# A streaming encoder layer on one core: other waits and priorities in the first norm, and spatial products of the v rows stepped later

## Chip, core and metric

The kernel runs on one core of a Trainium2 chip, as one program. The metric is the device time of an execution in microseconds; the kernel before takes 1891.32 us (median of 3 runs, 1890.37 to 1892.46). A core has a matmul engine (TensorE, called PE in the profile), VectorE (DVE), ScalarE (ACT), GpSimd (POOL) and SyncE (SP), each with its own queue of instructions, which it works off in order. They meet through semaphores. Matmuls write to PSUM, of which the kernel holds eight tiles of one bank; the other engines empty them.

## What is computed

One inference step of one layer for 1024 prompt rows and 32 sample rows, all in float32. Cut to what matters:

```python
x = layer_norm(x, ln_in_g, ln_in_b)
f = swiglu(modulate(x, 0), ffn1_w1, ffn1_w3, ffn1_w2)
x = layer_norm(ALPHA * x + 0.5 * gate(0) * f, ln_g[0], ln_b[0])      # the first norm

proj = modulate(x, 1) @ w_in
xa, ga, us, vs = jnp.split(proj, [D_LRU, 2 * D_LRU, 2 * D_LRU + D_SG], axis=-1)
xc, new_hist = causal_conv(xa, conv_hist, conv_w, conv_b)
hl, h_last = rg_lru(xc, h0, lru_wa, lru_ba, lru_wx, lru_bx, lru_lambda)
ya = hl * jax.nn.gelu(ga)
vn = layer_norm(vs, sg_ln_g, sg_ln_b)
yb = spatial_gate(us, vn, sg_w, sg_b)                                # us * (tril(w_s) @ vn + b_s)
m = jnp.concatenate([ya, yb], axis=-1) @ w_out
x = layer_norm(ALPHA * x + gate(1) * m, ln_g[1], ln_b[1])

f = swiglu(modulate(x, 2), ffn2_w1, ffn2_w3, ffn2_w2)
x = layer_norm(ALPHA * x + 0.5 * gate(2) * f, ln_g[2], ln_b[2])
```

`modulate` and `gate` scale and shift by vectors that come from c. The spatial gate works on blocks of 128 rows, in four groups of 128 columns. Outputs are the rows, the states of the convolution and of the recurrence, and the normalised v rows of the sample.

## The kernel before

**Layout.** Activations lie transposed, 128 features on the partitions, eight feature blocks k, and the 1056 rows along the free side in three chunks: 384, 384 and 288 (`CH`, indices 0 to 2). A float32 product is made of three matmuls with a high part and a low part of each operand: high by high, high by low, low by high. `split` (L209) makes such a pair: ACT copies the high part (L210), DVE or POOL subtracts it to get the low part (L211). One k of one chunk, three matmuls, is called a group here.

**Order.** PE's instructions run in the order in which the Python code issues them. The other engines' instructions are ordered by a planner, which takes each engine's ready instruction of the highest priority by its own estimate of durations; the priority is the place in the program, and `high_priority(offset=n)` moves an instruction n places forward in it.

**Side work.** Work beside the main products is written as generators. `self.pe` is a clock that counts the planned length of the matmuls issued so far: columns / 2.4 ns, so 0.16 us for 384 columns and 0.12 for 288, times four for a plain float32 product. `go` (L156) registers a generator with a due time; a yielded number is the time until its next step. `poll` (L162) steps the generators that are due. It is called behind every group of the main products, and in the v rows behind each row tile (24 matmuls of 512 columns). `drain` (L173) steps one generator at once to its end, or, with `out=True` and a norm, until its modulated rows are issued.

**The first norm.** `last_f` issues the last products of the first feed-forward net chunk by chunk: per chunk eight sets of nine matmuls, each emptied by `add_gated` (L960 adds to the residual rows, L966 to the running total `tot`). Behind each chunk it registers `ln` (L1189) for it. `ln` has four steps, with the waits of `STEPS[(1, chunk)]` ahead of the first, the second and the third product:

- the product `psl<-tot,ones`, which sums over the features; DVE subtracts the mean (L1202)
- then, if the chunk before has issued its modulated rows, ACT squares in two halves into two `t` tiles (L1210), and DVE adds up the squares (L1213, L1215, L1218)
- the products `psl<-ones,t`, the variance; L562 on DVE and L563 on POOL make the inverse root, L1232 a diagonal of it
- the last product `psl<-tot,ones`; DVE scales the rows (L1241), ACT scales and shifts by the coefficients (L539, into the same two `t` tiles) and makes the high part `xh` (L546), DVE the low part `xl` (L549), in four pairs of feature blocks; the rows are spilled to DRAM

The second tuple of `STEPS` holds the priorities of these four groups of instructions.

**The mix.** `mix` (L1502) then issues, chunk by chunk (`chunkwise`, L1535, which drains the norm of a chunk ahead of its first product), the products ga 0 to 3 and xa 0: 40 groups of chunk 0, 40 of chunk 1, 40 of chunk 2. Behind them come xa 1 and xa 2 (`whole`), then the v rows, xa 3, and again chunk by chunk us 0 to 3, whose eviction multiplies with `zb` (L1531). The products of `w_out` (wo) follow. Beside all this the generator `lru` runs the convolution and the recurrence, long DVE instructions over 1060 columns, with gate products `psg`; it is drained behind chunk 0 of us.

**The v rows.** Nine row tiles, three per chunk: 24 matmuls each, and ACT copies the result into a tile of the tag `v0` (L1595; the profile calls the tile `v`). `sgv` (L1461) normalises the three tiles of a chunk (L1471 to L1475), then for each splits it into `vhl`, a tile of the tag `raw`, and behind a wait issues twelve products `psz` with the spatial weights and evicts them into `zb` (L1492, four instructions). For the sample's tile it also loads two rows (L1497) and stores vn (L1500), through SP. `sgv` of a chunk is drained behind the first row tile of the next chunk, ahead of its copy, and the last one ahead of us.

The `raw` tag has five buffers. They hold the weight tiles that SP loads from DRAM (L205), and the tiles of `sgv` and `lru`.

Of the kernel before, what the change touches and what calls it, by code (L numbers as in the profile page):

```python
# [12 lines left out]
F32 = mybir.dt.float32  # L13
# [6 lines left out]
P = 128  # L20
# [20 lines left out]
for _n, _w in _COLS:  # L41
# [18 lines left out]

STEPS = {
# [61 lines left out]
class Core:  # L123
# [1337 lines left out]
    def sgv(self, c, v0):  # L1461

        nc, V, S, G = self.nc, self.nc.vector, self.nc.scalar, self.nc.gpsimd
        mv = self.mixl.tile([P, 3, 2], F32, tag="vmv", name="vmv", bufs=2)
        rs = self.mixl.tile([P, 3, 2], F32, tag="vrs", name="vrs", bufs=2)
        c0 = CH[c][0]
        rows = [P if c * 3 + j < 8 else NS for j in range(3)]
        for j in range(3):
            n = rows[j]
            bs = self.mixl.tile([P, 6], F32, tag="vbs", name="vbs", bufs=2)  # L1470
            V.bn_stats(bs[:n], v0[j][:n])  # L1471
            V.bn_aggr(mv[:n, j, :], bs[:n])
            self.rsqrt(rs[:n, j, 0:1], mv[:n, j, 1:2])
            V.scalar_tensor_tensor(rs[:n, j, 1:2], mv[:n, j, 0:1], -1.0, rs[:n, j, 0:1], ALU.mult, ALU.mult)
            S.activation(v0[j][:n], v0[j][:n], AF.Identity, scale=rs[:n, j, 0:1], bias=rs[:n, j, 1:2])  # L1475
        yield 6.0
        for j in range(3):
            n = rows[j]
            vh = self.wpool.tile([P, 2, 512], F32R, tag="raw", name="vhl", bufs=RAWS)
            self.split(vh[:n, 0, :], vh[:n, 1, :], v0[j][:n])  # L1480
            yield 2.0
            ps = self.ps("psz")
            for g in range(4):
                gs = slice(g * P, (g + 1) * P)
                o = ps[:, g * P:g * P + n]
                wg = slice(g * P, g * P + n)
                self.mm(o, vh[:n, 0, gs], self.wt[:n, 0, wg], True, False)
                self.mm(o, vh[:n, 0, gs], self.wt[:n, 1, wg], False, False)
                self.mm(o, vh[:n, 1, gs], self.wt[:n, 0, wg], False, True)
            tk = c0 + j * P  # L1490
            for g in range(4):
                V.scalar_tensor_tensor(self.zb[:, g, tk:tk + n], ps[:, g * P:g * P + n], self.v("sg_g", g),  # L1492
                                       self.R[:, g, :n], ALU.mult, ALU.add)
            if n == NS:
                r = self.wpool.tile([P, 1024], F32, tag="raw", name="raw", bufs=RAWS)
                for q, nm in ((0, "sglg"), (1, "sglb")):
                    nc.sync.dma_start(r[:NS, q * 512:(q + 1) * 512], self.i[nm].partition_broadcast(NS))  # L1497
                V.tensor_tensor(v0[j][:n], v0[j][:n], r[:NS, 0:512], ALU.mult)
                V.tensor_tensor(v0[j][:n], v0[j][:n], r[:NS, 512:1024], ALU.add)
                nc.sync.dma_start(self.o["vn"], v0[j][:n])  # L1500

    def mix(self, ln1, es_a, es_mr):  # L1502
# [5 lines left out]
        def new_xab(f, pool, bufs):  # L1508
            x = pool.tile([P, 1064], F32, tag="l", name="xab", bufs=bufs)
            nc.gpsimd.memset(x[:, 0:3], 0.0)  # L1510
            nc.gpsimd.memset(x[:, 1062:1064], 0.0)
            hist = self.v("hist").rearrange("p (r f) -> p r f", f=4)
            V.tensor_copy(x[:, 1027:1030], hist[:, :, f])
            xabs[f] = x
# [20 lines left out]
        def chunkwise(items, before=None, after=None):  # L1535
            ws = []
            for c in range(3):
                if before:
                    self.drain(before[c], True)
                for j, it in enumerate(items):  # L1540
                    if c == 0:
                        ws.append(self.w_get(it))
                        if it[0] == "xa":
                            new_xab(it[1], self.mixr, 1)
                    ps = self.ps()
                    for k in range(K):
                        self.h_mm(ps, ws[j], c, k, k == 0, k == K - 1)
                    outs[it[0]](it[1], c, ps)
                    if c == 2:
                        self.w_rel()  # L1550
                if after:
                    after(c)

        def whole(it):
            w = self.w_get(it)
            if it[0] == "xa":
                new_xab(it[1], self.mixl, 7)
            ps = [self.ps() for _ in range(3)]
            for k in range(K):
                for c in range(3):  # L1560
                    self.h_mm(ps[c], w, c, k, k == 0, k == K - 1)
            self.w_rel()
            for c in range(3):
                outs[it[0]](it[1], c, ps[c])
# [12 lines left out]
        whole(("xa", 2))  # L1577
        self.drain(sgc)
        wv = [self.w_get(("vs", j)) for j in range(4)]
        sg = None  # L1580
        for c in range(3):
            v0 = []
            for j in range(3):
                n = P if c * 3 + j < 8 else NS
                ps = self.ps()
                for k in range(K):
                    h, l = (x[c][:, k, j * P:j * P + n] for x in (self.xh, self.xl))
                    wh, wl = wv[k // 2][k % 2][:, 0], wv[k // 2][k % 2][:, 1]
                    self.mm(ps[:n, :], h, wh, k == 0, False)
                    self.mm(ps[:n, :], h, wl, False, False)  # L1590
                    self.mm(ps[:n, :], l, wh, False, k == K - 1)
                if j == 0 and sg:
                    self.drain(sg)
                t = self.mixl.tile([P, 512], F32, tag="v0", name="v0", bufs=3)
                S.activation(t[:n], ps[:n, :], AF.Copy)  # L1595
                v0.append(t)
                self.poll()
            sg = self.go(self.sgv(c, v0))
        self.w_rel(8)
        whole(("xa", 3))  # L1600
        self.drain(sg)

        def to_x(c):
            self.drain(lru)
            c0, n = CH[c]
            for h, src in ((0, self.ya), (1, self.zb)):
                sl = slice(4 * h, 4 * h + 4)
                self.split(self.xh[c][:, sl, :], self.xl[c][:, sl, :], src[:, :, c0:c0 + n])

        chunkwise([("us", j) for j in range(4)], after=to_x)  # L1610
        es_l.close()
        es_mr.close()
        self.apool, self.es_a2 = self.pool("a2", side="left")
# [130 lines left out]
```

## Time and profile before

| | |
|---|---|
| median of 3 runs | 1891.32 us (1890.37 to 1892.46) |
| the profiled execution | 1891.25 us |
| its span, first to last instruction | 1889.4 us |
| mean granted TensorE clock | 0.99 |
| PE in `ps<-xh,wh` products, the largest group | 901.7 us, 3824 matmuls |
| the chain that ended last | PE 83%, DVE 9%, POOL 3%, ACT 3%, DMA 1% |

The profile is of one execution. A line is read as line, engine, operation, output <- inputs, count; times in a timeline are microseconds from the start of the span, followed by the length, and in brackets stands the idle time ahead of an instruction and what ended it. PE's busy time is modelled from matmuls that overlap, so a busy PE need not run at its full rate: the granted clock says at which it ran (1.00 is full). The part of the span that the change touches lies between 770 us, where chunk 0 of the last feed-forward products ends, and 1040 us, where wo begins.

### The profile page before, as it was taken

What the parts mean: (1) busy time and instruction counts of PE and PEld (TensorE: products, weight loads), DVE (VectorE), ACT (ScalarE), POOL (GpSimd) and SP (SyncE); (2) the same over time, 40 slices, a digit from 0 to 9 for tenths busy, and PEclk for the clock granted to TensorE, in tenths of its full rate; (3) what the DMA queues carried; (4) which work ended last, traced back from release to release, by engine and by line L of the source; (5) the groups of instructions that cost most, each with busy time, mean ns of one, the idle gap of its engine ahead of it and who ended that gap; (6) DMA issues with size and microseconds to landing.
All of it is one profiled execution on the core that took longest, in us unless ns stands there. A gap on an engine that the chain in (4) does not pass through costs nothing.

```text
span 1889.4 us, 28312 instructions
## 1 busy us (share of the span) xinstructions
PE 1830.2 (97%) x11295; PEld 1793.0 (95%) x11295; DVE 1334.5 (71%) x2362; ACT 683.3 (36%) x1200; POOL 557.1 (29%) x416
## 2 busy tenths in 40 slices
PE   6989999999999999989999999999999999999997
PEld 3889999999999999979789999999999999999996
DVE  7889888878888866962977467965645554565667
ACT  5551332233223223344554437222232233223224
POOL 2493434233333424022000000133333233423410
PEclk9999999999999999989899999999999999999999
DMA  7351353445445433222011401111111112012102
GB/s 294 123 182 65 126 187 131 139 154 173 147 139 179 147 110 123 90 76 78 3 51 39 168 23 46 45 56 35 45 67 46 45 45 68 23 45 68 45 1 92
DMA packets 51028, 175.70 MB, mean 93 GB/s; under 512 B 7504, under 2 KB 10192, under 8 KB 50128
## 3 DMA queue, kind: packets, MB, share of 16 engines
q1 hardware_dynamic: 31984, 102.77, 16.1%
q10 hardware_dynamic: 18912, 71.11, 10.9%
q8 instruction: 89, 1.46, 0.3%
q14 instruction: 43, 0.35, 0.1%
HBM read 165.13 MB, written 8.74 MB: 92 GB/s over the span
## 4 chain that ended last, share of the span: by engine, by line
PE 83%; DVE 9%; POOL 3%; ACT 3%; DMA 1%; issue 1%; SPq 0%; ACTq 0%; DVEq 0%; POOLq 0%
PE ps L153 80%; PE psl L153 1%; DVE xl L549 1%; POOL s L801 1%; DVE wh L211 1%; DVE xa L960 1%; PE psz L153 1%; POOL tx L804 1%; PE psa L153 1%; DVE araw L714 1%; POOL s L802 1%; DMA araw<-ada 1%; PE psg L153 0%; POOL raw L242 0%; ACT wh L210 0%
## 5 line engine op out<-in xcount | busy, mean ns | idle before, releaser
L153 PE MATMUL ps<-xh,wh 128*128 128x384 f32 (+1 forms) x3824 | 901.7, 319 | 3.0 <-ACT xh L546 1.8
L153 PEld LDWEIGHTS ps<-xh,wh 128*128 128x128 f32 x3824 | 662.1, 188 | 6.6 <-ACT xh L546 2.0
L153 PE MATMUL ps<-xl,wh 128*128 128x384 f32 (+1 forms) x1912 | 608.2, 318 | 4.2 <-DVE xl L549 4.2
L210 ACT ACTIVATE wh<-raw 128x512 fp32r<-128x512 f32 x452 | 281.1, 628 | 587.7 <-PE ps L153 462.9
L153 PE MATMUL ps<-g,wh 128*128 128x384 f32 (+1 forms) x2808 | 459.6, 323 | 3.0 <-ACT g L210 1.3
L153 PEld LDWEIGHTS ps<-g,wh 128*128 128x128 f32 x2808 | 453.1, 188 | 5.0 <-ACT g L210 1.5
L211 DVE TENSOR_TENSOR wh<-raw,wh 128x512 fp32r<-128x512 f32 x283 | 215.1, 764 | 223.4 <-ACT wh L210 218.1
L153 PEld LDWEIGHTS ps<-xl,wh 128*128 128x128 f32 x1912 | 359.8, 188 | 7.6 <-DVE xl L549 6.5
L211 POOL TENSOR_TENSOR wh<-raw,wh 128x512 fp32r<-128x512 f32 x169 | 248.3, 1471 | 387.3 <-ACT wh L210 385.9
L960 DVE SCALAR_TENSOR_TENSOR xb<-ps,gt,xb 128x384 f32<-128x384 f32 (+1 forms) x352 | 151.4, 484 | 79.4 <-PE ps L153 65.1
L714 DVE SCALAR_TENSOR_TENSOR araw<-araw,cb 128x1024 f32<-128x1024 f32 x112 | 161.1, 1444 | 15.1 <-DMA araw<-ada 11.0
L153 PE MATMUL ps<-tx,wh 128*128 128x384 f32 x912 | 167.1, 338 | 0.0
L240 POOL TENSOR_TENSOR raw<-raw 128x512 f32<-128x512 f32 x38 | 54.5, 1434 | 365.7 <-DVE wh L211 361.0
L153 PEld LDWEIGHTS ps<-tx,wh 128*128 128x128 f32 x912 | 159.8, 188 | 0.0
L960 DVE SCALAR_TENSOR_TENSOR xa<-ps,gt,xa 128x384 f32<-128x384 f32 (+1 forms) x320 | 135.1, 479 | 8.5 <-PE ps L153 8.4
L210 ACT ACTIVATE g<-s 128x384 fp32r<-128x384 f32 (+1 forms) x126 | 61.3, 493 | 168.3 <-DVE s L675 168.2
L852 DVE TENSOR_TENSOR s<-s,ps 128x384 f32<-128x384 f32 x152 | 83.8, 551 | 41.4 <-PE ps L153 39.7
L211 DVE TENSOR_TENSOR g<-s,g 128x384 fp32r<-128x384 f32 (+1 forms) x126 | 93.5, 748 | 21.8 <-ACT g L210 20.8
L563 POOL TENSOR_TENSOR r<-r,half 128x3 f32<-128x3 f32 x8 | 7.1, 888 | 303.9 <-DVE r L562 303.9
L153 PE MATMUL ps<-T,wh 128*128 128x384 f32 x456 | 85.6, 335 | 0.0
L675 DVE TENSOR_TENSOR s<-s 128x384 f32<-128x384 f32 x76 | 59.0, 777 | 32.4 <-ACT s L902 31.4
L242 POOL TENSOR_TENSOR raw<-raw 128x512 f32<-128x512 f32 x38 | 55.7, 1465 | 87.3 <-DVE wh L211 85.9
(246 smaller groups left out, 1684.9 us busy)
## 6 DMA issues: line engine op xcount, KB each, us to landing
raw<-wst SPq DMA_DIRECT2D x156, 512.0 KB, 3.8
araw<-ada ACTq DMA_DIRECT2D x112, 512.0 KB, 3.5
wnat<-ada SPq DMA_DIRECT2D x8, 512.0 KB, 10.2
raw<-ada SPq DMA_DIRECT2D x8, 512.0 KB, 3.6
xt<-x SPq DMA_DIRECT2D x7, 512.0 KB, 8.4
araw<-wst ACTq DMA_DIRECT2D x6, 512.0 KB, 4.5
sp<-xa ACTq DMA_DIRECT2D x2, 1536.0 KB, 5.7
xb<-sp ACTq DMA_DIRECT2D x2, 1536.0 KB, 10.3
```

Source lines behind the costliest of these rows:

```text
L153: self.nc.tensor.matmul(out, a, b, start=start, stop=stop, skip_group_check=True)
L210: self.nc.scalar.activation(dst_h, src, AF.Copy)
L211: (e or self.nc.vector).tensor_tensor(dst_l, src, dst_h.bitcast(F32), ALU.subtract)
L240: G.tensor_tensor(a["A21"], a["A11"], a["A21"], ALU.subtract)
L242: G.tensor_tensor(a["A22"], a["A22"], a["A21"], ALU.subtract)
L549: V.tensor_tensor(xl, tmp, xh.bitcast(F32), ALU.subtract)
L675: self.nc.vector.tensor_tensor(s, s, x, ALU.mult)
L714: V.scalar_tensor_tensor(raws[n], raws[n], 1.0, cb, ALU.mult, ALU.mult, accum_out=self.mod[:, m, f, v:v + 1])
L801: e.tensor_tensor(r, x[i][:, k, :].bitcast(F32), y[i][:, k, :].bitcast(F32), op)
L802: e.tensor_tensor(t, t, u, ALU.add)
L852: self.mark = V.tensor_tensor(out, x, ps[:, :n], ALU.add)
L960: self.mark = V.scalar_tensor_tensor(X[:, m, a + o:a + o + w], ps[:, o:o + w], self.gt[:, s, m, v:v + 1], X[:, m, a + o:a + o + w], ALU.mu ...
```

## The change

It has four parts.

- `STEPS[(1, 1)]`: the variance of chunk 1 waits 14 instead of 12, and the subtraction of its mean has the priority offset 0 instead of 30.
- `STEPS[(1, 2)]`: the mean of chunk 2 waits 15 instead of 6, its last product 4.0 instead of 2.5.
- `sgv`: the wait behind the norm is 9.0 instead of 6.0, and the wait between a split and its products 4.5 instead of 2.0.
- `mix`: the tag `v0` has six buffers instead of three. `sgv` of a chunk is no longer drained behind the first row tile of the next chunk; from the third chunk on, that of the chunk before the last one registered is. Nothing is drained behind xa 3; instead `chunkwise` drains `sgv` of a chunk ahead of the us products of that chunk.

```diff
@@ -60,8 +60,8 @@
     (1, 0): ((1.2, 12.0, 4.0), (0, 30, 0, 0), 0),
-    (1, 1): ((4.0, 12.0, 4.0), (30, 30, 0, 30), 0),
-    (1, 2): ((6.0, 12.0, 2.5), (0, 0, 30, 0), 0),
+    (1, 1): ((4.0, 14.0, 4.0), (0, 30, 0, 30), 0),
+    (1, 2): ((15.0, 12.0, 4.0), (0, 0, 30, 0), 0),
@@ -1473,12 +1473,12 @@
             S.activation(v0[j][:n], v0[j][:n], AF.Identity, scale=rs[:n, j, 0:1], bias=rs[:n, j, 1:2])
-        yield 6.0
+        yield 9.0
         for j in range(3):
             n = rows[j]
             vh = self.wpool.tile([P, 2, 512], F32R, tag="raw", name="vhl", bufs=RAWS)
             self.split(vh[:n, 0, :], vh[:n, 1, :], v0[j][:n])
-            yield 2.0
+            yield 4.5
             ps = self.ps("psz")
@@ -1577,7 +1577,7 @@
-        sg = None
+        sgs = []
         for c in range(3):
@@ -1589,17 +1589,15 @@
-                if j == 0 and sg:
-                    self.drain(sg)
-                t = self.mixl.tile([P, 512], F32, tag="v0", name="v0", bufs=3)
+                if j == 0 and len(sgs) > 1:
+                    self.drain(sgs[-2])
+                t = self.mixl.tile([P, 512], F32, tag="v0", name="v0", bufs=6)
                 S.activation(t[:n], ps[:n, :], AF.Copy)
                 v0.append(t)
                 self.poll()
-            sg = self.go(self.sgv(c, v0))
+            sgs.append(self.go(self.sgv(c, v0)))
         self.w_rel(8)
         whole(("xa", 3))
-        self.drain(sg)
@@ -1607,7 +1605,7 @@
-        chunkwise([("us", j) for j in range(4)], after=to_x)
+        chunkwise([("us", j) for j in range(4)], before=sgs, after=to_x)
```

## The prediction

> **What bounds the kernel now.** I read the page first, then the waits of TensorE, then windows around the longest of them, then the timelines of the engines inside those windows.
>
> ```profile
> span 1889.4 us, 28312 instructions
> PE 1830.2 (97%) x11295; PEld 1793.0 (95%) x11295; DVE 1334.5 (71%) x2362; ACT 683.3 (36%) x1200; POOL 557.1 (29%) x416
> ```
>
> PE is busy 97% of the span, so only two things can be won: its 59 us of idle time (1889.4 - 1830.2), and stretches in which it is "busy" but slow. The waits of PE between 700 and 1060 us (total, times, longest) show what lies in the stage that the change touches:
>
> ```profile
> PE psl L153 <- DVE tot L966: 4.5, 1, 4.5
> PE psz L153 <- DVE vhl L211: 3.7, 3, 2.7
> PE ps L153 <- DVE xl L549: 2.4, 3, 1.3
> PE psz L153 <- ACT vhl L210: 0.8, 1, 0.8
> PE psl L153 <- DVE t L1218: 0.7, 1, 0.7
> ```
>
> The first, third and fifth belong to the first norm, the others to the v rows. The windows (length; busy of PE, PEld, DVE, ACT, POOL; granted clock; DMA share; GB/s) show that each long wait costs a second time:
>
> ```profile
> 801.84:812.54 10.70, 8.32 (x44) 7.04 (x42) 10.70 (x22) 8.06 (x10) 5.93 (x3) 1.00 0.15 50
> 812.54:817.05 4.51, 0.00 (x0) 0.00 (x0) 4.51 (x6) 0.03 (x1) 3.68 (x3) 0.87 0.32 116
> 817.05:826.35 9.30, 9.30 (x31) 9.01 (x31) 3.27 (x5) 0.49 (x1) 0.85 (x1) 0.51 0.18 56
> 927.82:933.21 5.39, 1.88 (x16) 1.60 (x14) 5.28 (x10) 4.41 (x6) 0.00 (x0) 0.88 0.01 2
> 933.21:942.00 8.79, 8.79 (x32) 7.92 (x33) 8.10 (x18) 1.34 (x2) 0.55 (x1) 0.50 0.00 0
> ```
>
> After the idle 4.51 us the clock stands at 0.51 for 9.30 us, which is worth 9.30 x 0.49 = 4.6 us; after the psz waits at 0.50 for 8.79 us, 4.4 us. The three xl waits (2.4 us, spread over the first window) left it at 1.00. DVE is full in the first two windows: there the norm waits for VectorE's queue, not for its own length.
>
> **The norm, step by step.** The planner's clock counts 0.16 us for a matmul of 384 columns and 0.12 for 288; the chip takes (next start minus start, over 24) 0.173:
>
> ```profile
> 749.80 4.32 PE L153 MATMUL ps<-tx,wh 128*128 128x384 f32 x24
> 753.96 2.25 PE L153 MATMUL ps<-T,wh 128*128 128x384 f32 x12
> 801.84 0.34 PE L153 MATMUL ps<-xh,wh 128*128 128x384 f32 x1
> 836.71 0.35 PE L153 MATMUL ps<-xh,wh 128*128 128x384 f32 x1
> ```
>
> The last two rows start chunks 0 and 1 of the ga/xa products: 34.87 us for 120 matmuls, which need 20.8 us plus about 1.3 for the norm's own products. So 12.8 us are lost here; 2.4 + 4.5 + 4.6 = 11.5 of them are named above, and the other 1.3 are slow restarts behind the short waits, which I leave to the low end of the range.
>
> *Priority 30 to 0 for the mean subtraction (L1202) of chunk 1.* These DVE and ACT rows show what it did:
>
> ```profile
> 797.80 1.75 DVE L1202 SCALAR_TENSOR_TENSOR xa<-psl,xa 128x1536 f32<-128x1536 f32 x1
> 799.83 1.75 DVE L1202 SCALAR_TENSOR_TENSOR xa<-psl,xa 128x1536 f32<-128x1536 f32 x1
> 802.81 0.95 DVE L549 TENSOR_TENSOR xl<-t,xh 128x768 fp32r<-128x768 f32 x1
> 807.25 0.95 DVE L549 TENSOR_TENSOR xl<-t,xh 128x768 fp32r<-128x768 f32 x1
> 803.79 1.49 ACT L1210 ACTIVATE t<-xa 128x1536 f32<-128x1536 f32 x1 [2.99 <-DVE xl L549]
> 808.23 1.49 ACT L1210 ACTIVATE t<-xa 128x1536 f32<-128x1536 f32 x1 [0.66 <-DVE xl L549]
> ```
>
> Both L1202 go ahead of the second and fourth xl of chunk 0, though their own squares (L1210) cannot start before exactly these: the two "t" tiles are free only when xl has read them. So the priority gained the norm nothing and made PE wait. Without it the second xl can follow the first L1202 at 799.5, the fourth can be done near 804, and the squares near 802.3 and 805.5. Nothing is added; 2.4 us go.
>
> *Waits.* In planner time the mean of chunk 1 stands 4.68 us into the products of chunk 2, and chunk 0 of ga/xa starts at 9.28. Its variance moves from 16.68 to 18.68: behind group 20 of 40 (a group is three matmuls, 0.48), which is 801.84 + 60 x 0.173 = 812.2 us. Its last product, 4.0 later, comes behind group 27 or 28, at about 816.8. The mean of chunk 2, which now waits 15 instead of 6, comes behind group 30 (818.4); its variance behind group 14 or 15 of chunk 1, its last product (4.0 instead of 2.5) behind group 22. The total that PE waited for ended at 817.0:
>
> ```profile
> 781.18 0.55 DVE L1218 TENSOR_TENSOR t<-t,t 128x384 f32<-128x384 f32 x1
> 815.18 1.45 DVE L1218 TENSOR_TENSOR t<-t,t 128x384 f32<-128x384 f32 x1
> 816.55 0.44 DVE L966 TENSOR_TENSOR tot<-tot,xa 128x288 f32<-128x288 f32 x1
> 806.61 6.64 POOL L211 TENSOR_TENSOR wh<-raw,wh 128x512 fp32r<-128x512 f32 x3 [18.30 <-ACT wh L210]
> 813.21 3.01 POOL L211 TENSOR_TENSOR wx<-raw,wx 128x512 fp32r<-128x512 f32 x2
> ```
>
> At 818.4 it is there even if DVE is no faster: 4.5 and the 4.6 of slow clock go. What is late next is the variance at 812.2, which needs L1218 of chunk 1. From squares done at 805.5 three sums follow; at the slow lengths that they have while POOL splits weights (L1218: 1.45 against 0.55) they take about 4.5 us, so 810, or 813 with two totals between them. I take no stall; the other end is the rival below.
>
> *The next chunk comes sooner.* Chunk 0 now ends near 823.9, and its cover over the modulation of chunk 1 shrinks. Before, the last product and the four xl stood so:
>
> ```profile
> 827.22 0.81 PE L153 MATMUL psl<-tot,ones 128*128 128x384 f32 x2
> 832.52 0.96 DVE L549 TENSOR_TENSOR xl<-t,xh 128x768 fp32r<-128x768 f32 x1 [1.04 <-ACT xh L546]
> 837.87 0.96 DVE L549 TENSOR_TENSOR xl<-t,xh 128x768 fp32r<-128x768 f32 x1 [0.52 <-ACT xh L546]
> ```
>
> The first xl is done 6.3 us behind the product, the last 11.6. Counted from 816.8: 823.1 and 828.4. PE asks for the first at 823.9 and for the last 3.1 us later, 827.0. So about 1.5 us of short waits are new; bounds 0 and 4.1 (the two halves of chunk 2's L1202 between them, 2.6 together). Chunk 2's last product keeps some 10 us before its chunk, about what its modulation needs; no cost. The L1218 wait of 0.7 stays: its squares also wait for those xl. **Norm: 2.4 + 4.5 + 4.6 - 1.5 = 10.0 us.**
>
> **The v rows.** The 108 psz matmuls, their splits and evictions stay; their places move. Before, chunk 0's were forced behind the first row tile of chunk 1, at 927.82, when DVE was full with the recurrence and still evicting and splitting:
>
> ```profile
> 931.44 1.12 DVE L1492 SCALAR_TENSOR_TENSOR zb<-psz,vec,R 128x128 f32<-128x128 f32 x4
> 932.47 1.28 DVE L211 TENSOR_TENSOR vhl<-v,vhl 128x512 fp32r<-128x512 f32 x2
> 946.58 0.69 DVE L1471 BATCH_NORM_STATS2 vbs<-v 128x6 f32<-128x512 f32 x1
> 933.21 4.96 PE L153 MATMUL psz<-wt,vhl 128*128 128x128 f32 x22 [2.73 <-DVE vhl L211]
> 956.50 4.13 PE L153 MATMUL psz<-wt,vhl 128*128 128x128 f32 x36
> ```
>
> Now they are forced behind the first row tile of chunk 2, three tiles later: each is 24 matmuls of 512 columns, 5.12 us of planner time or 5.5 at 0.173 for 0.16, so 944.3 on the old scale. The recurrence's scan block ended there at 946.58; without twelve evictions of 0.28 (3.3 us) ahead of it, near 943, and only three splits of 0.64 then stand before psz, each due 1.3 us behind the last. The second group of 36, in the same place in the code, ran without a wait (last row), under a less full DVE. So 0.8 + 3.7 of waits and 4.4 of slow clock go; I take 0.4 for a late split, with bounds 0 and the whole 8.9. Chunks 1 and 2 are stepped by the planner, 4.5 us between split and product, among the xa 3 and us products; what is not done is forced ahead of the us chunk that reads it. Three more v tiles only let ACT empty PSUM sooner. A split now holds a "raw" buffer until its product, and with the last one go two small loads and the store of vn on SP's queue, ahead of weight loads:
>
> ```profile
> 995.65 0.34 SPq L1500 DMA_DIRECT2D vn<-v  x1
> 996.08 0.87 SPq L205 DMA_DIRECT2D raw<-wst  x2
> 1029.63 0.34 SPq L1623 DMA_DIRECT2D st<-st  x1
> raw<-wst SPq DMA_DIRECT2D x156, 512.0 KB, 3.8
> ```
>
> The store comes some 12 us later by the planner's steps, and so the two loads of wo, near 1008; SP's next issue stood 33 us behind them, so I cost this at nothing. Were that cover gone, PE would wait for one landing, 3.8 us (the page's list of issues), and one split, 1.3. **v rows: 4.5 + 4.4 - 0.4 = 8.5 us.**
>
> **Sum.** The profiled execution took 1891.25 us (span 1889.4; median of the runs 1891.32). 1891.25 - 10.0 - 8.5 = **1872.8 us**.
>
> [...]
>
> **Rivals.**
> *The variance takes the total's place.* L1218 ends at 816.6 as before, because DVE's work from 790 to 817 us is the limit and POOL's five splits (9.65 us) now fall on the sums. PE idles from 812.2 to 816.6 and the clock falls again. Won is only what PE does sooner: 18 matmuls (3.1 us) and 0.45; chunk 0 is then long enough to cover the modulation. 1891.25 - 3.6 - 8.5 = 1879.2. For it: DVE is 100% busy there. Against: squares 2.7 us sooner. [...]
> *The forced products still wait.* If splits come behind the scan, psz waits as before, with its slow clock; only the last two waits (1.0) go: 1891.25 - 10.0 - 1.0 = 1880.3.
> *Slower: the last products of the norm are forced at the chunk borders.* If the longer waits carry them to group 40, chunk 1 starts with the whole modulation open: the last xl 11.6 us later, of which 3.1 are covered, plus 4.6 of slow clock, 13.1 us; chunk 2 the same, as its modulation is no shorter: 26.2 - 18.5 = 7.7 slower, 1899. It decides from group 40; my count says 28 and 22.
> *It does not do what it says.* VectorE's order is a planner's, with its own durations; if it leaves L1202 and the splits where they were, both refills above come together, and more: 1887 to 1892.
>
> **Chances.** Forecast 0.64 (own range 1869 to 1877), variance 0.16, forced products 0.08, no real move 0.07, slower 0.05. The range reaches from 1869 (nothing new late, the 1.3 of restarts gone too) to 1880.5, past the first two rivals, and leaves out 0.17 with the tails. 0.2%, 3.8 us, is about what a measurement of this kernel can tell from none: faster 0.88, same 0.07, slower 0.05.
>
> **What would show it.** PE's waits on tot and on xl in chunk 0 gone, the clock at 1.00 from 790 to 950 us, chunk 0 about 22 us long; short xl waits at the start of chunk 1; 36 psz in a row behind 24 matmuls of the third v chunk. A wait on L1218 of over 3 us behind group 20, or a window at 0.5, shows the rivals. Wrong would be all of it if an idle stretch of several us stood elsewhere.

## The result, and the profile after

Over the repeated runs the kernel with the change takes 1878.65 us (median, 1877.25 to 1881.03) and the kernel before 1890.84 us beside it: a ratio of 0.9939 with an interval of 0.9925 to 0.9953. It is faster by 12.2 us, two thirds of the 18.5 that were forecast. That is inside the stated range, though outside the 1869 to 1877 that the prediction gave to its forecast alone. The summary of its profiled execution (1877.9 us):

```profile
span 1876.1 us, 28307 instructions
PE 1823.0 (97%) x11295; PEld 1784.8 (95%) x11295; DVE 1329.9 (71%) x2362; ACT 684.0 (36%) x1200; POOL 556.2 (30%) x416
```

The span is 13.3 us shorter. To say where, I cut the TensorE timeline at instructions that both kernels have: the first product of each chunk of ga/xa, the first of the v rows, and the second norm's first sum (`psl<-tot,ones`). Four of these rows, of the kernel before and then of the changed kernel (start, length, engine, instruction):

```profile
902.73 0.63 PE L153 MATMUL ps<-wh,xh 128*128 128x512 f32 x2
1105.66 0.48 PE L153 MATMUL psl<-tot,ones 128*128 128x384 f32 x1
```

```profile
799.75 0.34 PE L153 MATMUL ps<-xh,wh 128*128 128x384 f32 x1
827.06 0.35 PE L153 MATMUL ps<-xh,wh 128*128 128x384 f32 x1
893.70 0.40 PE L153 MATMUL ps<-wh,xh 128*128 128x512 f32 x1
1090.79 0.48 PE L153 MATMUL psl<-tot,ones 128*128 128x384 f32 x1
```

Chunk 0 lasts from 799.75 to 827.06, 27.31 us, where it lasted 34.87; the part from the v rows to the second norm 197.09 (1090.79 - 893.70), where it lasted 202.93. Chunk 1 went from 23.08 to 23.26, chunk 2 from 15.97 to 16.41. So the norm brought 7.56 - 0.18 - 0.44 = 6.9 us and the v rows 5.8. The rest lies where nothing was changed: the first norm's first sum was issued at 770.72 and not at 772.80 (2.1 us won), and from 1834 us on some 1.5 us were lost at a lower granted clock (0.57 over 1834 to 1838 us; the kernel before reads 1.00 from 1820 to 1870). Such differences are an execution's own; this is why stages are compared below.

TensorE's waits in the changed kernel, 700 to 1060 us (total, times, longest):

```profile
PE ps L153 <- DVE xl L549: 3.0, 5, 1.2
PE psz L153 <- DVE vhl L211: 1.6, 1, 1.6
PE ps L153 <- DVE zb L1492: 1.5, 1, 1.5
PE psl L153 <- DVE t L1218: 1.2, 1, 1.2
```

The wait on the total (4.5) is gone and so are the old waits on vhl (3.7 and 0.8). But xl is waited for no less than before (2.33 us of it in chunk 0), and vhl, zb and L1218 have waits of their own. The windows over chunk 0 (length; busy of PE, PEld, DVE, ACT, POOL; granted clock; DMA share; GB/s):

```profile
799.75:806.18 6.43, 4.11 (x22) 3.10 (x20) 6.43 (x10) 3.81 (x6) 1.12 (x1) 1.00 0.00 0
806.18:814.75 8.57, 7.38 (x41) 7.08 (x42) 8.57 (x12) 4.78 (x6) 8.01 (x5) 1.00 0.36 123
814.75:819.67 4.92, 4.92 (x31) 4.92 (x31) 1.02 (x4) 0.49 (x1) 0.85 (x1) 1.00 0.33 110
```

The clock stands at 1.00 in all three: the stretch at 0.51 is gone. VectorE is full until 814.75, when TensorE stops waiting for L1218. Its timeline says why, with a ScalarE row and GpSimd's five splits:

```profile
797.55 1.75 DVE L1202 SCALAR_TENSOR_TENSOR xa<-psl,xa 128x1536 f32<-128x1536 f32 x1
799.58 1.75 DVE L1202 SCALAR_TENSOR_TENSOR xa<-psl,xa 128x1536 f32<-128x1536 f32 x1
801.25 0.95 DVE L549 TENSOR_TENSOR xl<-t,xh 128x768 fp32r<-128x768 f32 x1
805.17 0.95 DVE L549 TENSOR_TENSOR xl<-t,xh 128x768 fp32r<-128x768 f32 x1
808.53 1.49 DVE L1213 TENSOR_TENSOR t<-t 128x768 f32<-128x768 f32 x1
811.42 1.64 DVE L1215 TENSOR_TENSOR t<-t 128x384 f32<-128x384 f32 x1
813.14 1.47 DVE L1218 TENSOR_TENSOR t<-t,t 128x384 f32<-128x384 f32 x1
```

```profile
795.36 0.83 ACT L546 ACTIVATE xh<-t 128x768 fp32r<-128x768 f32 x1
```

```profile
805.06 2.68 POOL L211 TENSOR_TENSOR wh<-raw,wh 128x512 fp32r<-128x512 f32 x1 [18.83 <-ACT wh L210]
807.70 1.51 POOL L211 TENSOR_TENSOR wh<-raw,wh 128x512 fp32r<-128x512 f32 x1
809.17 2.01 POOL L211 TENSOR_TENSOR wh<-raw,wh 128x512 fp32r<-128x512 f32 x1
811.14 1.50 POOL L211 TENSOR_TENSOR wx<-raw,wx 128x512 fp32r<-128x512 f32 x1
812.61 1.59 POOL L211 TENSOR_TENSOR wx<-raw,wx 128x512 fp32r<-128x512 f32 x1
```

The xh of the second pair is there at 796.2, yet both L1202 still go ahead of its xl (801.25), as before. Counted from the first product of chunk 0, the priority taken away did move the first L1202: it begins 2.20 us ahead of that product where it began 4.04 ahead. But what passed it were additions of chunk 2, and not xl; the kernel with the priority alone has the same 2.20. The last three sums fall on GpSimd's five splits and end at 814.6, which is 14.9 us into the chunk; in the kernel before it was 14.8 (815.18 + 1.45 - 801.84). So the sums came no sooner at all.

### The profile page after: what moved, and what is told of

Read it like the earlier page. It is cut to its first block, busy times and chain, and to the rows that moved or that the text cites. A ratio compares the mean times of both kernels' runs of the same rounds, so it can differ in the third digit from the quotient of the medians.

```text
span 1876.1 us, 28307 instructions
## 1 busy us (share of the span) xinstructions
PE 1823.0 (97%) x11295; PEld 1784.8 (95%) x11295; DVE 1329.9 (71%) x2362; ACT 684.0 (36%) x1200; POOL 556.2 (30%) x416
## 4 chain that ended last, share of the span: by engine, by line
PE 81%; DVE 10%; ACT 3%; POOL 3%; issue 1%; DMA 1%; SPq 0%; ACTq 0%; DVEq 0%; POOLq 0%
PE ps L153 79%; DVE xl L549 1%; PE psl L153 1%; DVE wh L211 1%; POOL s L801 1%; ACT t L539 1%; DVE xa L960 1%; PE psa L153 1%; POOL tx L804 1%; DVE araw L714 1%; POOL s L802 1%; POOL tx L803 0%; ACT xh L546 0%; DVE s L801 0%; POOL raw L242 0%
## 5 line engine op out<-in xcount | busy, mean ns | idle before, releaser
L153 PEld LDWEIGHTS ps<-T,wh 128*128 128x128 f32 x456 | 80.2, 188 | 0.0
## 6 DMA issues: line engine op xcount, KB each, us to landing
wnat<-ada SPq DMA_DIRECT2D x8, 512.0 KB, 10.2
```

Source lines behind the costliest of these rows:

```text
L153: self.nc.tensor.matmul(out, a, b, start=start, stop=stop, skip_group_check=True)
```

## The experiments

A small table of stage lengths first, each from the profiled execution of its kernel as above (us; "v" is from the v rows to the second norm). Ratios are to the kernel before, with 95% intervals. How far one execution can be trusted shows in rows whose v rows are the same code: 201.91 to 203.19 us for those of the kernel before, 197.09 to 200.18 for those of the changed kernel. The last section has the reason.

| kernel | chunk 0 | chunks 1, 2 | v | ratio |
|---|---|---|---|---|
| before | 34.87 | 23.08, 15.97 | 202.93 | 1 |
| changed | 27.31 | 23.26, 16.41 | 197.09 | 0.9939 (0.9925 to 0.9953) |
| norm part alone | 27.31 | 23.26, 16.42 | 203.19 | 0.9964 (0.9952 to 0.9976) |
| v rows part alone | 34.83 | 23.08, 15.96 | 197.11 | 0.9977 (0.9966 to 0.9987) |
| priority alone | 33.66 | 23.09, 15.97 | 201.91 | 0.9991 (0.9981 to 1.0001) |
| norm's waits alone | 27.43 | 23.23, 16.41 | 202.79 | 0.9979 (0.9964 to 0.9994) |
| L1202 behind xl | 27.35 | 23.30, 16.41 | 200.18 | 0.9941 (0.9928 to 0.9953) |
| splits on VectorE | 25.87 | 23.25, 16.42 | 198.64 | 0.9931 (0.9916 to 0.9946) |
| no forced step | 27.29 | 23.26, 16.41 | 196.75 | 0.9933 (0.9919 to 0.9946) |
| vhl in a tag of its own | 28.88 | 23.23, 16.41 | 204.04 | 0.9979 (0.9970 to 0.9988) |
| order by hand | 23.87 | 23.29, 16.41 | 197.09 | 0.9924 (0.9909 to 0.9940) |
| order, splits, no forced step | 22.92 | 23.31, 16.42 | 195.25 | 0.9911 (0.9897 to 0.9925) |
| splits, no forced step | 25.86 | 23.25, 16.42 | 195.20 | 0.9920 (0.9908 to 0.9932) |
| sgv's waits as before | 27.30 | 23.23, 16.40 | 205.41 | 0.9995 (0.9986 to 1.0004) |

### Each half alone

The first has only the two lines of `STEPS` changed, the second everything but these.

> The STEPS rows of the change alone; the v rows as before. Theory: the two parts are independent, and the norm's is worth what the traces show of it, chunk 0 of ga/xa from 34.9 to 27.3 us and 0.6 given back in the next chunks: 6.9 us, 0.37% (ratio 0.9963). Rival: the parts depend on each other, since the recurrence's DVE work starts when the norm ends; then this run and e2_vrows together differ from the change's 12 us by more than 3.

> The v rows' part of the change alone; STEPS as before. Theory: 5.9 us, 0.31% (ratio 0.9969): the waits of 4.5 us and the 8.8 us at half clock behind row tile 3 are gone, and two new waits stand, 1.6 us of psz on vhl in xa 3 and 1.5 us of ps on zb behind the forced products. Rival: as in e1_norm.

Measured were 0.9964 and 0.9977; their product, 0.9941, is the change's 0.9939. In the traces the halves bring 6.7 and 5.9 us, together 12.5 of the change's 12.8. So the halves are independent, and each fell short by itself.

### Priority alone, waits alone

```diff
-    (1, 1): ((4.0, 12.0, 4.0), (30, 30, 0, 30), 0),
+    (1, 1): ((4.0, 12.0, 4.0), (0, 30, 0, 30), 0),    # first kernel
+    (1, 1): ((4.0, 14.0, 4.0), (30, 30, 0, 30), 0),   # second kernel, which has (1, 2) as in the change
```

> Only the priority offset of chunk 1's mean subtraction (L1202), 30 to 0; all waits as before. The prediction: the three xl waits (2.4 us) go, ratio 0.9987. Theory now: in the trace of after both L1202 still stand ahead of the second xl, because the planner holds L1202 for ready first, so the offset is worth nothing: the waits on xl and on tot stay, ratio 1.000 within 0.0008.

> Only the waits of STEPS (14, 15, 4.0), priority offset 30 as before. Theory: the whole gain of the norm, 6.9 us (ratio 0.9963), as e1_norm. If the offset matters, this is slower than e1_norm by some 2 us.

The priority alone is worth nothing that can be told (0.9991, the interval reaches past 1): xl is waited for 2.3 us and the next sum 4.6, as before; its shorter chunk 0 is a shorter stretch of slow clock (the last section has its windows). The waits alone bring the whole of the norm's part in the trace (27.43 against 27.31). Their median is 2.5 us above that of the kernel with the norm part alone, which takes the priority away too, but the two intervals overlap, so the ratios do not decide whether the priority is worth something beside the waits. In the trace the waits alone get there otherwise: L1218 is not waited for, but the clock fell. The window behind the third xl wait of the kernel with the waits alone:

```profile
808.07:815.00 6.93, 6.93 (x31) 6.93 (x32) 6.93 (x10) 4.30 (x6) 6.93 (x5) 0.75 0.36 118
```

0.25 of 6.93 us, 1.7, went to the clock after xl waits of only 0.56, 0.47 and 1.33. The prediction had said that three such waits leave it at 1.00. That this costs chunk 0 nothing has a reason: L1218 ends 14.8 us into the chunk here too (14.9 in the changed kernel), and a TensorE that comes late by its slow clock merely waits less for it.

### L1202 put behind xl, in two ways

If the two L1202 are what makes xl late, a hand-written order should win the 2.3 us that the priority did not. The first kernel holds only the two L1202 behind the second and the fourth xl and the squares behind the last xh:

```diff
+                with tc.issue_after(self.xls[(-3, -1)[h]].ins) if (s, c) == (1, 1) else nullcontext():
                 V.scalar_tensor_tensor(X[:, H[h], :], ps[:, :n].unsqueeze(1).to_broadcast([P, 4, n]), -1.0 / D,
...
+                with tc.issue_after(self.xhs[-1].ins) if (s, c) == (1, 1) else nullcontext():
                 S.activation(t[:, :, :n], X[:, H[h], :], AF.Square)
```

> The changed kernel, with the order that the prediction took for granted put in by hand: the two halves of chunk 1's L1202 queue behind the second and the fourth xl of chunk 0, and its squares behind the last xh. Prediction's mechanism: both xl waits of chunk 0 (2.3 us) go, and the variance (L1218, 1.2 us of wait) is no later, so chunk 0 falls from 27.3 to about 23.5 us and the time by 3 to 4 us against the change (about 0.9920 of the kernel before). Rival: DVE's total work is the limit, so what xl gains the sums lose: the wait on L1218 grows to about 3 us and the time stays within 1 us of the change's.

It missed: chunk 0 took 27.35 us. The time is the one that the rival named, though L1218 was waited for only 0.24 us and not 3. In the gap that L1202 left, the planner put the additions of chunk 2, and the second xl began 1.26 us into the chunk (801.77), hardly sooner than in the changed kernel (1.50). xl was still waited for 0.85 and 1.22 us (VectorE's timeline of this kernel):

```profile
801.80 1.15 DVE L966 TENSOR_TENSOR tot<-tot,xa 128x288 f32<-128x288 f32 x1
803.03 0.94 DVE L549 TENSOR_TENSOR xl<-t,xh 128x768 fp32r<-128x768 f32 x1
```

So it is not L1202 as such that delays xl: when L1202 is held back, something else takes the place. That the planner takes xl to be ready later than it is, and so gives its place to whatever else is ready, is argued from the order alone; its estimates were not read. Behind the second xl wait the clock fell in this execution as well (0.76 over 7.04 us, 1.7 us lost), and L1218 ended 14.9 us into the chunk once more, so chunk 0 is as long as in the changed kernel. The second kernel holds these additions back too:

```diff
+                with self.tc.issue_after(self.xls[(-3, -3, -2, -2, -1, -1)[m - 2]].ins) if pc == PIECES[-1] and m > 1 else nullcontext():
                 self.add_gated(ps, 0, pc, m, tot)
```

> The changed kernel with VectorE's and ScalarE's order of the first norm put in by hand: each of the second to fourth xl of chunk 0 stands ahead of the additions (L960, L966) of the last sets of chunk 2 and ahead of the two subtractions of the mean (L1202), and the third and fourth xh stand ahead of the squares (L1210). Theory, late xl are a matter of VectorE's order: the xl waits of chunk 0 (2.3 us after the change) go, and chunk 0 of ga/xa falls from 27.3 to 24 to 25.5 us; the L1218 wait (1.2 us) stays or changes by less than 1 us. Rival, VectorE has no time left in that stretch, so that order only moves the wait: the xl waits go, and L1218 or the total (tot L966, behind group 30) is late by as much, chunk 0 stays at 27 to 28 us. Ratio by the theory 0.9925, by the rival 0.994.

VectorE's timeline and the windows over chunk 0, which begins at 800.17:

```profile
796.70 0.95 DVE L549 TENSOR_TENSOR xl<-t,xh 128x768 fp32r<-128x768 f32 x1
798.57 0.96 DVE L549 TENSOR_TENSOR xl<-t,xh 128x768 fp32r<-128x768 f32 x1
801.64 1.52 DVE L549 TENSOR_TENSOR xl<-t,xh 128x768 fp32r<-128x768 f32 x1
811.05 0.54 DVE L1218 TENSOR_TENSOR t<-t,t 128x384 f32<-128x384 f32 x1
```

```profile
800.17:811.74 11.57, 10.60 (x63) 10.31 (x61) 11.57 (x15) 7.44 (x10) 6.86 (x5) 1.00 0.38 137
811.74:824.04 12.30, 12.30 (x71) 11.93 (x71) 9.29 (x14) 5.19 (x9) 1.05 (x1) 1.00 0.01 1
```

Nobody waits for xl in chunk 0 any more and chunk 0 takes 23.87 us; 0.97 of waiting for L1218 is left. L1218 itself ends at 811.6, 11.4 us into the chunk, where it had ended 14.9 into it. The rival, that VectorE has no time left, falls: in another order L1218 ends 3.4 us sooner. Two things in the trace bring this about beside the place of xl. Two more totals of chunk 2 (L966) now stand behind L1218, and GpSimd's splits begin at 799.73, ahead of the chunk, and stretch three of VectorE's instructions (L549 1.52 us, L966 1.55, L1213 1.63) instead of five (L966 1.00 and 1.55, L1213 1.49, L1215 1.64, L1218 1.47). And the 3.4 us are just what chunk 0 is shorter (27.31 - 23.87). In the changed kernel it was therefore the end of L1218 that set the length of chunk 0: without the xl waits TensorE would only have waited longer for it.

### Five splits on VectorE in place of GpSimd

`window` is the flag under which GpSimd makes the low part of a weight split.

```diff
-                    self.window = True
+                    self.window = False
```

> The changed kernel with POOL taken out of the weight splits behind the norm: the low parts go to DVE. Theory: the sums of chunk 1 are slow because POOL reads SBUF beside them; without it L1213, L1215 and L1218 last about 0.95, 0.55 and 0.55 us instead of 1.49, 1.64 and 1.47, and five splits of 0.65 more stand on DVE; L1218 ends about when it does now or 1 to 2 us sooner, so the time is within 2 us of the change's. Rival: DVE's operations are slow for a reason of their own (length of the queue, PSUM): then they stay at 1.5 us, and five splits later the wait on L1218 is 4 us.

With GpSimd idle, the last three sums, though VectorE has the five splits to do as well (three ahead of these sums, two behind):

```profile
809.70 0.95 DVE L1213 TENSOR_TENSOR t<-t 128x768 f32<-128x768 f32 x1
810.73 0.55 DVE L1215 TENSOR_TENSOR t<-t 128x384 f32<-128x384 f32 x1
811.57 0.55 DVE L1218 TENSOR_TENSOR t<-t,t 128x384 f32<-128x384 f32 x1
```

0.95, 0.55 and 0.55 in place of 1.49, 1.64 and 1.47. L1218 ends 11.0 us into the chunk and is not waited for, and chunk 0 is 1.4 us shorter; the xl waits of 2.3 us stay. That the splits on GpSimd are what stretches the sums is shown by this run.

### The forced step behind the seventh row tile

In the changed kernel the psz of v chunk 0 wait for nothing, but the row tile behind them waits 1.49 us for zb. Without the forced step the planner places all psz of that chunk:

```diff
-                if j == 0 and len(sgs) > 1:
-                    self.drain(sgs[-2])
```

> The changed kernel without the forced psz of chunk 0 in the v rows; the planner steps them between the row tiles. Theory: the wait of ps on zb (1.5 us) comes from three psz and six psg tiles in a row, with the evictions behind DVE's other work; spread, it goes: 1.5 us less than the change. The wait of psz on vhl in xa 3 (1.6 us) stays. Rival: the evictions are late anyway, and the wait shows up at another tile.

In the changed kernel, VectorE empties the three psz tiles late, behind the statistics of the next v tile, which wait for its copy, and TensorE gets the tile that it needs when two of them are empty (VectorE, then TensorE):

```profile
938.85 0.69 DVE L1471 BATCH_NORM_STATS2 vbs<-v 128x6 f32<-128x512 f32 x1 [1.43 <-ACT v L1595]
940.74 1.12 DVE L1492 SCALAR_TENSOR_TENSOR zb<-psz,vec,R 128x128 f32<-128x128 f32 x4
942.90 2.16 DVE L1492 SCALAR_TENSOR_TENSOR zb<-psz,vec,R 128x128 f32<-128x128 f32 x8
```

```profile
944.07 0.50 PE L153 MATMUL ps<-wh,xh 128*128 128x512 f32 x1 [1.49 <-DVE zb L1492]
```

Without the forced step the zb wait goes; in place of the 1.63 for vhl stand 0.98 and 0.56 at the same place. In this execution the clock also fell behind them. The stretch here, and in the kernel with the splits on VectorE and no forced step, which has the same code there:

```profile
970.30:979.00 8.70, 8.14 (x44) 8.00 (x45) 7.37 (x21) 4.36 (x9) 0.97 (x1) 0.80 0.14 49
```

```profile
966.87:975.60 8.73, 8.17 (x58) 8.03 (x59) 7.93 (x22) 4.58 (x10) 0.97 (x1) 1.00 0.13 46
```

That is 0.2 x 8.70 = 1.7 us, about the difference between 196.75 and 195.20. Where the clock holds, the forced step costs 1.9 us (197.09 - 195.20). The intervals of the ratios (0.9939 and 0.9933) are wider than that, so only the stages show it.

### vhl away from the weights' buffers

```diff
-            vh = self.wpool.tile([P, 2, 512], F32R, tag="raw", name="vhl", bufs=RAWS)
+            vh = self.mixl.tile([P, 2, 512], F32R, tag="vhl", name="vhl", bufs=1)
```

Without the forced step either.

> e7_nodrain with a buffer of its own for vhl instead of one of the five raw buffers. Theory: the wait on vhl in xa 3 is a wait for a raw buffer (ACT's copy of vhl stood 4.2 us behind the splits of the us weights that held them); with its own buffer it goes, 1.6 us less than e7_nodrain. Rival: DVE's queue of eight weight splits and the recurrence makes it late; then the wait stays at 1 us or more.

It took 1886.92 us beside 1877.75 with the `raw` buffers: TensorE waited 5.3 us in four places (0.97, 2.01, 0.72, 1.60), and behind two of these waits the clock fell (0.67 over 10.25 us and 0.77 over 7.58, together 5.1 us). A single vhl must be read before the next split can begin. So the run tells what one buffer costs, and not whether vhl waits for a `raw` buffer in the changed kernel. ScalarE's copies for vhl do stand behind weight splits there:

```profile
964.71 1.15 ACT L210 ACTIVATE vhl<-v 128x512 fp32r<-128x512 f32 x2 [4.23 <-DVE wh L211]
```

That these copies wait for a buffer stays argued; no run had two vhl of their own, or six `raw` buffers.

### The waits of sgv as before

```diff
-        yield 9.0
+        yield 6.0
...
-            yield 4.5
+            yield 2.0
```

> The changed kernel with the waits of sgv as before (6.0 and 2.0 in place of 9.0 and 4.5); its buffers and the places of its forced steps stay as changed. Theory, what helped the v rows is that the products of v chunk 0 are forced three row tiles later: the 36 psz of chunk 0 still stand there and wait no more than 1 us for vhl, the v rows take 197 to 198 us, ratio 0.994. Rival, the longer waits are what helped (splits have time before their products): psz waits on vhl of 3 us or more come back among the later products, the v rows take 200 us or more, ratio 0.996.

The rival won as to the v rows: their gain is lost whole, 205.41 us where the kernel before has 202.93. The ratio of 0.9995 is worse than the rival's 0.996. In the trace chunk 0 to the second norm is 4.5 us shorter than in the kernel before, but this execution lost 3.8 us ahead of the chunk and 1.5 us behind the second norm, where the code is the same; whether the others lost as much has no trace and stays open. TensorE's longest wait in this kernel, 700 to 1060 us, the windows from it on, and the VectorE row that ends it:

```profile
PE psz L153 <- DVE vhl L211: 7.0, 1, 7.0
```

```profile
967.11:974.12 7.01, 0.01 (x1) 0.00 (x0) 6.22 (x21) 2.25 (x3) 1.07 (x2) 0.72 0.00 1
974.12:983.00 8.88, 8.88 (x44) 8.88 (x45) 4.18 (x12) 1.26 (x2) 0.00 (x0) 0.65 0.00 1
```

```profile
973.40 1.87 DVE L211 TENSOR_TENSOR vhl<-v,vhl 128x512 fp32r<-128x512 f32 x3
```

And the same row of the changed kernel:

```profile
967.56 1.87 DVE L211 TENSOR_TENSOR vhl<-v,vhl 128x512 fp32r<-128x512 f32 x3
```

The v rows of this kernel begin here:

```profile
899.53 0.63 PE L153 MATMUL ps<-wh,xh 128*128 128x512 f32 x2
```

So the split stands 73.87 us into them; in the changed kernel 967.56 - 893.70 = 73.86. VectorE does it at the same place in both. What differs is when TensorE asks: 67.6 us into the v rows here, 73.0 there (its wait of 1.63 ended at 968.29). The 5.4 us between are the difference of the waits, 7.01 - 1.63; 0.35 x 8.88 = 3.1 of slow clock come on top. Together 8.5, where the stage is 8.3 longer. It is the only psz wait here: the four of the kernel before are gone in this kernel too. So the new places and buffers took those away, and the longer waits keep this one small. The longer waits without the new places were not run.

### A version faster than both

> The changed kernel with the five splits on VectorE and without the forced step, the planner's own order kept. Each alone measured 0.9931 and 0.9933. If the two are independent and the second is worth nothing, chunk 0 is 25.9 us, the v rows 196 to 198 us, ratio 0.993; if the second were worth its wait of 1.5 us, 0.9925.

The splits on VectorE and no forced step: 0.9920, whose interval (0.9908 to 0.9932) holds both expectations; the stages, 25.86 and 195.20 us, say that the two add up where the clock holds. The v rows came out shorter than the 196 to 198 us expected. With the hand-written order as well:

> The order of the run before, and five weight splits on VectorE in place of GpSimd, and no forced step of sgv behind the first row tile of the third v chunk. Theory: the three sums of squares take 0.95, 0.55 and 0.55 us as they do when GpSimd is idle, neither xl nor L1218 is waited for, chunk 0 is 22.5 to 24 us, and the v rows stay within 1 us of the change's; ratio 0.991 to 0.992. Rival, the five splits (3 to 4 us of VectorE) push the additions and xl later again: chunk 0 is no shorter than 25.5 us, ratio 0.993.

The theory held for chunk 0 and for the ratio; the v rows, 195.25 us, are 1.8 us shorter than the change's and not within 1. It took 1874.46 us beside 1890.54, a ratio of 0.9911 (0.9897 to 0.9925), whose interval ends where the change's begins. Against the hand-written order alone (0.9924) and the splits without forced step (0.9920) the ratios do not tell it apart; the stages do. In the trace its stages from chunk 0 to the second norm are 6.2 us shorter than the changed kernel's. Chunk 0, one window:

```profile
805.78:828.70 22.92, 22.92 (x133) 22.26 (x132) 21.61 (x33) 12.64 (x19) 1.05 (x1) 1.00 0.20 70
```

PE is busy for all of its 22.92 us at clock 1.00. This is close to the 22.1 that the prediction counted as needed.

## Why the prediction was right in sign and a third too large

The forecast was 1872.8 us. The measured 1878.65 lies close to the 1879.2 of the first rival, and that closeness is luck: the rival had 3.6 us for the norm and 8.5 for the v rows, the stages show 6.9 and 5.8.

**The wait on the total: right.** It was to go with its slow clock, 4.5 + 4.6, once the mean of chunk 2 stood near group 30. It went, with waits alone as well, and chunk 0 is shorter by 7.6.

**The step that failed in the norm: "Without it the second xl can follow the first L1202 at 799.5, the fourth near 804".** The second xl started at 801.25 and the fourth at 805.17. The priority did not put L1202 behind xl; 2.33 of the 2.4 us stayed. I took a lower priority for an order. That was not all: with L1202 put behind xl by hand, as the step has it, chunk 0 still took 27.35 us, because additions took the place. Only with these held back too did it come to 23.87 us, where 34.87 - 11.5 = 23.4 was forecast, with a norm gain of 11.0 - 0.2 - 0.4 = 10.4 against the 10.0 forecast. So VectorE had the time that the prediction saw, but neither the priority nor the order of L1202 alone frees it.

**"I take no stall" at the variance: wrong, and by more than the 1.2 us of its wait.** The second square was to be done sooner; it began 6.4 us into the chunk, as before, since it waited for the fourth xl (5.4 us in, as before), and the sums then met GpSimd's splits. L1218 was forecast to end 8 to 11 us into the chunk and ended 14.9 into it. That is the mechanism of the rival "the variance takes the total's place", which has L1218 end as before. Its wait was 1.2 us and not 4.4 only because TensorE, held up by the xl waits and their restarts (0.28 us from the first matmul behind a wait to the next, where others take 0.17 to 0.18), asked 13.8 us into the chunk and not at the 10.4 forecast; and the clock held. The two causes were separated: another order alone lets L1218 end at 11.4, splits on VectorE alone at 11.0. By TensorE's idle time chunk 0 won 7.56 in place of 11.5 for 2.33 of xl, 1.20 of L1218 and a rest of 0.4 that no run splits up.

**The cost at the next chunks: over-sized.** 1.5 us was taken, 0.18 + 0.44 measured; the new xl waits there are 0.3 and below. Two readings were wrong beside it: the L1218 wait of 0.7, which was to stay, is gone, and chunk 2, costed at nothing, took the 0.44. The sum also let chunk 0 end at 823.9, with 1.3 us of restarts gone that it does not book.

**The v rows: mechanism right, one term mis-sized.** The old waits and their slow clock (8.9) went. The term "0.4 for a late split" measured 3.1: 1.49 for zb and 1.63 for vhl; 8.9 - 3.1 = 5.8 is what the stage won. The zb wait was not in the sum at all: I counted that splits are ahead of psz, not that 36 psz in one place fill three PSUM tiles whose emptying stands behind VectorE's other work. The vhl wait belongs to chunk 1, "stepped by the planner, 4.5 us between split and product", which I passed over. The run with the waits of sgv as before shows that this wait is not a detail: without the longer waits it is 7.0 us. The prediction gave the whole gain to the new places; without the longer waits these gain nothing here.

**"At nothing" for the buffers and SP's queue.** TensorE's waits from 700 to 1060 us show no cost of it, and the `raw` buffers stay open.

**The clock.** "The three xl waits left it at 1.00" held in the kernel before and not with the waits alone (0.75 over 6.93 us). The 9.30 and 8.79 us count from where TensorE goes on; the clock stood at 0.50 for 10.2 us each time, of which the first 1.1 and 1.2 lay in the idle time. The last section has the rows.

## What to carry to other kernels

A priority is not an order: before a gain is booked on it, look in the trace at what stands ahead of the instruction, and if its place matters, write the order out, for everything that can take the place. A wait that goes is a gain only if the next input is there sooner too: ask of each wait what TensorE would meet next. A product that is issued sooner than its input's place in another engine's queue gains nothing and costs the difference (7.01 us of wait for vhl here, 1.63 when it was issued later), so move the request to where the input stands. Read each stage by itself: executions differ by some us where nothing was changed (the v rows of one code took 197.09 to 200.18 us).

## What the hardware showed that was not expected

**The same wait lowers the clock in one execution and not in another.** Behind the wait of 1.63 us for vhl, in the changed kernel and then in the one with the splits on VectorE, whose code there is the same:

```profile
968.29:977.00 8.71, 8.71 (x64) 8.71 (x65) 7.27 (x14) 2.93 (x7) 0.00 (x0) 1.00 0.05 15
```

```profile
968.23:976.94 8.71, 8.71 (x51) 8.71 (x52) 5.75 (x13) 2.40 (x6) 0.00 (x0) 0.80 0.05 15
```

At 0.80, 1.7 us are lost over 8.71, which is half clock for 3.5 us (0.50 is what the clock reads all through the stretches that finer windows show below); the kernel with the norm's waits alone lost 1.7 over 6.93, the same. And the kernel with a tag for vhl, whose chunk 0 is in code and waits the changed kernel's, lost 1.7 us behind the wait on L1218:

```profile
817.84:831.72 13.88, 13.88 (x71) 13.51 (x71) 7.56 (x9) 5.24 (x9) 0.85 (x1) 0.88 0.12 39
```

So one execution's chunk 0 of 27.3 us is another's of 28.9. The kernel with L1202 behind xl, whose v rows are the changed kernel's code, lost 1.7 us behind the wait on zb (0.73 over 6.42) and 1.7 behind the one on vhl (0.76 over 7.07); that is its 200.18. **The slow stretches come in lengths of about 3.4, 6.8 and 10.2 us, the idle time counted in.** The kernel with the priority alone, its wait for the sum and what follows:

```profile
811.55:816.18 4.63, 0.01 (x1) 0.03 (x1) 4.57 (x6) 0.06 (x1) 3.71 (x3) 0.94 0.35 114
816.18:834.54 18.36, 18.36 (x88) 17.81 (x89) 8.90 (x9) 7.84 (x13) 0.85 (x1) 0.83 0.14 51
```

The loss is 0.06 x 4.63 + 0.17 x 18.36 = 3.4 us, at half clock 6.8 us. The kernel before, from the two pairs of windows shown in the prediction: 0.13 x 4.51 + 0.49 x 9.30 = 5.1, so 10.3 at half clock, and 0.12 x 5.39 + 0.50 x 8.79 = 5.0, so 10.1. The kernel with sgv's waits as before: 0.28 x 7.01 + 0.35 x 8.88 = 5.1, so 10.1. The short drops above: 3.3 to 3.5. In windows of 0.25 us the clock of the kernel before goes from 1.00 to 0.50 at 815.9 and back at 826.2, and again at 932.0 and 942.2, 10.2 us each; in the changed kernel it stands at 0.50 from 1834.1 to 1837.5, 3.4 us, behind a wait of 1.30 for L1218. The lengths are to each other about as one, two and three. In the two long stretches TensorE was busy from the end of its wait on (817.05 and 933.21), for 9.1 and 9.0 us, before the clock was back. What decides between one and three, and why one wait of 1.6 us lowers the clock in one execution and not in the next, was not shown.

**A sum on VectorE beside a split on GpSimd took 0.5 to 1.1 us longer, and ended just behind the split.** Undisturbed the three sums took 0.95, 0.55 and 0.55 us, beside the splits 1.49, 1.64 and 1.47. In the rows of the changed kernel, the splits that ran when these sums began ended at 809.21, 812.64 and 814.20; the sums ended at 810.02, 813.06 and 814.61, that is 0.81, 0.42 and 0.41 later, less than their undisturbed lengths. What holds a sum up while the split runs was not shown.
